# The low part of a weight used last in the projections and feed-forward products, and a doubled hand-over margin in the list scheduler

## The chip, the core and the metric

The kernel is one launch on one NeuronCore of a Trainium2 chip. Its engines are TensorE (PE for its matmuls, PEld for its weight loads), VectorE (DVE), ScalarE (ACT), GpSimd (POOL) and SyncE (SP), whose queue issues all of the kernel's transfers. The metric is the device time of the launch in microseconds (us); lower is better. A profiled execution also gives a span, from the first to the last instruction of the program.

## The reference

One decoder layer on 2048 tokens of width 1024 (DEPTH is 1, so only the first, gated-DeltaNet layer is computed):

```
proj = x @ w_in                       # q, k, v, z (8 heads of 128 each), 16 gate columns, 4 memory-query heads
qkv  = silu(causal_depthwise_conv(qkv)); q, k l2-normalised
o    = chunk_gated_delta_rule(q, k, v, g, beta)      # per head: a triangular solve per chunk, a state 128x128
o    = rms_norm(o) * silu(z);  m = memory_attention(mq, mem_k, mem_v)   # 256 memory tokens
x    = layer_norm(ALPHA * x + concat(o, m) @ w_out, ln1)
x    = layer_norm(ALPHA * x + square(relu(x @ w_ff1)) @ w_ff2, ln2)     # hidden width 4096
```

## The kernel before

**Arithmetic.** Each large product is made of three matmuls in a rounded fp32 type. An operand is split into a high part (a rounded copy, a CAST on ACT) and a low part (the original minus that copy, a subtraction on DVE). With `wh`, `wl` for a weight and `Thi`, `Tlo` for the transposed activations, one term of a product is Thi·wh + Tlo·wh + Thi·wl, all summed into the same PSUM bank. The low part of a weight is therefore ready only after its high part: transfer, CAST on ACT, subtraction on DVE. `hilo` and `hilo_in` (around line 465) do that for weights; the tiles come from a pool of 11 buffers with the tag `w`. The helper `mm3` issues the three matmuls in this order:

```
        nc.tensor.matmul(o, lh, rh, start=start, stop=False, **kw)
        nc.tensor.matmul(o, lh, rl, start=False, stop=False, **kw)
        nc.tensor.matmul(o, ll, rh, start=False, stop=stop, **kw)
```

**Stages.** The 2048 tokens go in four blocks of 512. In a block the mixer runs over ten steps: `dense` projects q, k, v, z of one head (accumulators `aq`, `ak`, `av`, `az`, each 24 matmuls of 512 columns, in `project`), `gdn_a` builds and inverts the chunk matrices (small plain-fp32 products `pkq`, `pq`, `pp`), `gdn_b` runs the state recurrence (`pc`, `po`) of the head before; `mem_proj` and `mem_attn` (`amq`, `sps`, `pmT`, `pmo`) do the memory heads. `out_proj` (accumulators `ao`) is interleaved at the end of the mixer. Then `norm1` normalises 128 tokens at a time (DVE, with a power on POOL), and `to_T` or `to_quads` transposes them (PE, tile `pt`) and splits them.

**Feed-forward.** The two feed-forward products (FF1, FF2; accumulators `af`) are done by a recursion of the Strassen kind: seven products of quarter size instead of eight, over sums and differences of quarters (`S1` to `S4`, `T1` to `T4`). Four groups of 1024 hidden units (`g`) each do FF1 and then FF2 for the block. In block 0 FF1 is plain (`ff1_tiles`, through `project`), and the sums of weights are made and kept in DRAM; in blocks 1 to 3 FF1 is `ff1_quads`, whose `step` does one of the seven products of 256 columns for two halves `i`. FF2 is the loop over `SEVEN` with the inner function `part(t, v)`; there the activations are the stationary operand (`xh`, `xl`, `hq`) and the weight is the moving one.

**Order.** The code above only records operations. `Recorder.issue` then plans: a list scheduler with one clock for each engine takes the recorded operation that can start first, ties by a priority that is the recording order (with hand-set shifts), and gives each an assumed duration. When an operation hands over to another engine, the reader is taken to be ready `LAT_FROM[e] + MARGIN` ns after the end of the writer, and a freed buffer is taken to be free as much later. `MARGIN` is 50. The planned start times only set the order in which the instructions are emitted on each engine; on the chip every engine runs its own list in order and waits on semaphores where a value is not there yet. Matmuls into the same bank stay in recorded order.

Of the kernel before, what the change touches and what calls it, by code (L numbers as in the profile page):

```python
# [14 lines left out]
P = 128  # L15
# [3 lines left out]
KT = D // P  # L19
# [13 lines left out]
RATE, FROM_SP, TO_SP = 330.0, 400, 400  # L33
LAT = {("PE", "PE"): 0, ("DVE", "DVE"): 120, ("ACT", "ACT"): 140, ("POOL", "POOL"): 100}
LAT_FROM = {"PE": 200, "DVE": 130, "ACT": 140, "POOL": 90, "SP": FROM_SP}
MARGIN = 50
SHIFT = 110
LATE = 600
PT3, PT2, PT1, PT4, PT5 = 0, 60, 30, 200, 130
# [28 lines left out]
class Ref:  # L68
# [58 lines left out]
    def part(self, *keys):  # L127
        return Ref(self.buf, self.shape, self.steps, frozenset(keys), self.p0)
# [223 lines left out]
def hybrid_layer(  # L352
# [24 lines left out]
    nc = tc.nc  # L377
# [59 lines left out]
    nc = rec  # L437
# [231 lines left out]
            nc.shift = 0  # L669

    def project(o, w, T, n=TB, t0=0):
        for k in range(KT):
            kk = [100 * k + t for t in range(t0 // P, (t0 + n) // P)]
            mm3(o, w[0][k], w[1][k], T[0][:, k, t0:t0 + n].part(*kk), T[1][:, k, t0:t0 + n].part(*kk),
                k == 0, k == KT - 1)


    mem_T = {}
# [515 lines left out]
    def ff_seven(b, ff1_tiles, ff1_quads, relu2, add, norm2):  # L1194
# [3 lines left out]
        for g in range(NS):  # L1198
            u0 = 4 * g
            X = [None] * 4  # L1200
# [72 lines left out]
            for n, (xn, wn, bn, on, (th, nh)) in enumerate(SEVEN[i] for i in order):  # L1273
                if not on:
                    banks[bn] = [bank("af2", ("ga%d" % t) if bn == "A" else "pb") for t in range(2)]
                w = [None, None]
                if b == NB - 1 and last and n == 5:
                    W = [rec.buf(tp, (P, 4, 1024), F32R, c, 1, "w") for c in ("Thi", "Tlo")]
                    spare.extend([x[:, i].part(("w", i)) for x in W] for i in range(4))

                def part(t, v):
                    if w[v] is None:
                        w[v] = as_rows(*(
                            hilo_in(tsc[u0 + v, wn]) if wn in (1, 2, 3, 4) else
                            hilo_in(fcp[u0 + v, wn]) if b else hilo(load_raw(row_part(u0 + v, wn)))))
                    for j in range(2):
                        k = 2 * v + j
                        h, l = X[k][xn]
                        mm3(banks[bn][t], h[:, t * P:(t + 1) * P], l[:, t * P:(t + 1) * P],
                            w[v][0][:, j], w[v][1][:, j], k == 0 and not on, k == 3, skip_group_check=on)  # L1290

                tail = last and n == len(SEVEN) - 1
                for v, t in ((0, 0), (1, 0), (0, 1), (1, 1)) if tail else ((0, 0), (0, 1), (1, 0), (1, 1)):
                    part(t, v)
                    if v:
                        add(2 * th + t, nh, banks[bn][t])
                        if tail:
                            norm2((t,), gb)
                if last and xn == "S1":
                    norm2((2, 3), gb)  # L1300
                if last and n < 4:
                    next_block(b + 1, n)
                if last and n == 5:
                    next_block(b + 1, 4)
# [46 lines left out]
    for b in range(NB):  # L1351
# [115 lines left out]
        def ff1_quads(vs, As, Bs, Cs, put):  # L1467

            out, held = {}, {}

            def step(v, n):
                wn, tn, bn, on = FF1_SEVEN[n]
                hi, lo = load_hilo(fhl[v, wn]) if (v, wn) in fhl else hilo_in((fsc if wn[0] == "S" else fac)[v, wn])
                hi, lo = (r.rearrange("p (a k f) -> p a k f", a=2, k=4) for r in (hi, lo))
                for i in range(2):
                    if bn == "A":
                        o, start = As[v, i][:, :256], not on
                    else:
                        o, start = (Bs if bn == "B" else Cs)[v][:, 256 * i:256 * i + 256], i == 0 and not on
                    for k in range(4):  # L1480
                        th, tl = quad_k(T1, tn, k)
                        for m, (a, x) in enumerate(((hi, th), (hi, tl), (lo, th))):
                            nc.tensor.matmul(o, a[:, i, k], x, start=start and k == 0 and m == 0,
                                             stop=k == 3 and m == 2, skip_group_check=True)
                    reads.append((v, n, i, o))

            def read(v, n, i, o):
                wn = FF1_SEVEN[n][0]
                if wn == "A12":
                    held[v, i] = o  # L1490
                    return
                if (v, i) not in out:
                    t, u = tok_tile("sq2"), tok_tile("ss4")
                    out[v, i] = t.rearrange("p (q f) -> p q f", q=4), u.rearrange("p (q f) -> p q f", q=4)
                a, st = out[v, i]
                sq = lambda q: a[:, q].part(q)
                ss = lambda q: st[:, q].part(q)
                sub = lambda o, x, y, op=ALU.subtract: nc.vector.tensor_tensor(out=o, in0=x, in1=y, op=op)
                if wn in ("A11", "S2", "S3"):
                    nc.scalar.copy(out=sq({"A11": 3, "S2": 1, "S3": 0}[wn]), in_=o)  # L1500
                    if wn != "A11":
                        return
                    o = held.pop((v, i))
                q = {"A11": 3, "S1": 0, "A22": 1, "S4": 2}[wn]
                if wn == "S4":
                    nc.scalar.activation(sq(q), o, AF.Relu)
                else:
                    nc.vector.tensor_tensor(out=sq(q), in0=sq(q), in1=o, op=ALU.add)
                    nc.scalar.activation(sq(q), sq(q), AF.Relu)
                nc.scalar.activation(sq(q), sq(q), AF.Square)  # L1510
                if wn == "S1":
                    put(v, i, ("A11", "A22"), a[:, 0:4:3].part(0, 3))
                elif wn == "A22":
                    sub(ss(0), sq(1), sq(3), ALU.add)
                    sub(ss(2), sq(0), sq(1))
                    sub(ss(1), ss(0), sq(0))
                    put(v, i, ("S3",), st[:, 2:3].part(2))
                    put(v, i, ("S1", "S2"), st[:, 0:2].part(0, 1))
                elif wn == "S4":
                    put(v, i, ("A12",), a[:, 2:3].part(2))  # L1520
                    sub(ss(3), sq(2), ss(1))
                    put(v, i, ("S4",), st[:, 3:4].part(3))

            order = [(v, n) for v in vs for n in range(7)]
            if len(vs) > 1:
                order.sort(key=lambda x: (x[1] > (x[0] == vs[0]), x[0], x[1]))
            reads = []
            for v, n in order:
                step(v, n)
                for q in reads:  # L1530
                    read(*q)
                reads.clear()
                if n == 6:
                    yield v
# [72 lines left out]
```

## Time and profile before

| | |
|---|---|
| median of 3 runs | 2855.46 us (2853.58, 2864.53, 2855.46) |
| the profiled execution | 2857.76 us |
| its span | 2855.8 us |
| PE, PEld busy in the span | 2817.9 us, 2420.0 us |
| DVE, ACT, POOL busy | 2341.8 us, 1648.5 us, 425.2 us |
| matmul records | 15869 |
| mean granted TensorE clock | 0.998 |

The profiled execution is 2.3 us above the median; 2.0 us of it lie outside its span. The profile's line for nearly every instruction is that of one helper (L335, where the recorded operations are emitted), so groups are told apart by the names of the tiles: `af<-wl,xh` is a matmul that writes `af` and reads `wl` and `xh`. The duration that a row gives for a matmul is its way through the pipeline; matmuls overlap, so the distance between two starts says what one costs in a row of them.

### The profile page before, as it was taken

The page shows a single profiled execution, that of the slowest core. Times are in us where ns is not written, and L with a number is a line of the kernel's source. Part 1 is how long each engine was busy: PE and PEld are TensorE (multiplying, and loading weights), DVE is VectorE, ACT ScalarE, POOL GpSimd, SP SyncE. Part 2 cuts the span into 40 slices and gives each one's busy share as a digit, 9 for nine tenths or more (in the row PEclk, how much of TensorE's full clock was granted, in tenths as well). Part 3 has the DMA queues.
Part 4 walks back from the last instruction along what each step waited for, and adds up shares of the span by engine and source line. Part 5 has one row for each costly group of instructions (what it writes and reads, how often), then busy time and mean ns, then how long its engine had stood idle before and what let it go on. Part 6 is the DMA issues. An engine that isn't in the chain of part 4 may idle for free. (4 is left out here: it accounts for less than half of the span.)

```text
span 2855.8 us, 47712 instructions
## 1 busy us (share of the span) xinstructions
PE 2817.9 (99%) x15869; PEld 2420.0 (85%) x15869; DVE 2341.8 (82%) x6188; ACT 1648.5 (58%) x4147; POOL 425.2 (15%) x1051
## 2 busy tenths in 40 slices
PE   9999999999999999999999999999999999999998
PEld 7888788888788888899988888889998888888997
DVE  8999989888889887777788986677788888577778
ACT  6677625555466663566645664256674666356664
POOL 2333200000133321000012321000002332000000
PEclk9999999999999999999999999999999999999999
DMA  8575569888877777655684434565577443465554
GB/s 300 209 264 188 176 220 312 297 283 270 299 259 257 237 257 266 218 187 188 217 270 152 133 122 148 210 207 188 188 236 250 132 141 121 166 237 177 188 188 177
DMA packets 200982, 609.59 MB, mean 213 GB/s; under 512 B 22560, under 2 KB 41376, under 8 KB 200352
## 3 DMA queue, kind: packets, MB, share of 16 engines
q1 hardware_dynamic: 200736, 606.55, 63.0%
q8 instruction: 125, 2.05, 0.3%
q14 instruction: 121, 0.99, 0.1%
HBM read 500.49 MB, written 127.99 MB: 220 GB/s over the span
## 5 line engine op out<-in xcount | busy, mean ns | idle before, releaser
L335 ACT CAST wh<-wl 128x1024 fp32r<-128x1024 f32 x334 | 349.7, 1048 | 246.2 <-DMA wl<-tsc 77.3
L335 DVE TENSOR_TENSOR wl<-wl,wh 128x1024 fp32r<-128x1024 f32 x334 | 400.0, 1219 | 62.2 <-ACT wh L335 62.1
L335 PE MATMUL af<-wh,xl 128*128 128x512 f32 x880 | 342.9, 390 | 1.3 <-DVE xl L335 1.3
L335 PE MATMUL af<-Thi,wh 128*128 128x256 f32 (+1 forms) x1056 | 323.5, 307 | 2.1 <-DVE tq L335 2.1
L335 PE MATMUL af<-Thi,wl 128*128 128x256 f32 (+1 forms) x1056 | 323.6, 307 | 1.3 <-DVE wl L335 1.3
L335 PE MATMUL af<-Tlo,wh 128*128 128x256 f32 (+1 forms) x1056 | 323.4, 306 | 0.0
L335 PE MATMUL af<-wl,xh 128*128 128x512 f32 x754 | 295.3, 392 | 3.6 <-DVE wl L335 3.5
L335 PE MATMUL af<-wh,xh 128*128 128x512 f32 x754 | 286.2, 390 | 2.3 <-ACT wh L335 2.2
L335 DVE SCALAR_TENSOR_TENSOR y<-y,af 128x512 f32<-128x512 f32 x224 | 151.0, 682 | 87.2 <-PE af L335 87.1
L335 PEld LDWEIGHTS af<-Thi,wh 128*128 128x128 f32 x1056 | 202.2, 192 | 12.3 <-DVE tq L335 2.8
L335 PEld LDWEIGHTS af<-Thi,wl 128*128 128x128 f32 x1056 | 202.4, 192 | 10.4 <-DVE wl L335 1.7
L335 PEld LDWEIGHTS af<-Tlo,wh 128*128 128x128 f32 x1056 | 202.4, 192 | 9.1
L335 PE MATMUL af<-Tx,wh 128*128 128x256 f32 x1152 | 209.3, 283 | 0.0
L335 ACT CAST wh<-wr 128x1024 fp32r<-128x1024 f32 (+1 forms) x132 | 136.9, 1038 | 121.9 <-DMA wr<-in_w_ff_dram 45.5
L335 PEld LDWEIGHTS af<-wh,xl 128*128 128x128 f32 x880 | 165.2, 188 | 35.8 <-DVE xl L335 1.7
L335 PEld LDWEIGHTS af<-Tx,wh 128*128 128x128 f32 x1152 | 179.8, 192 | 0.6 <-ACT sq L335 0.6
L335 PEld LDWEIGHTS af<-wl,xh 128*128 128x128 f32 x754 | 141.6, 188 | 38.5 <-DVE wl L335 9.9
L335 DVE TENSOR_TENSOR wl<-wr,wh 128x1024 fp32r<-128x1024 f32 (+1 forms) x132 | 158.5, 1203 | 16.7 <-ACT wh L335 12.6
L335 PEld LDWEIGHTS af<-wh,xh 128*128 128x128 f32 x754 | 141.4, 188 | 33.0 <-ACT wh L335 3.4
L335 PE MATMUL af<-Tx,wl 128*128 128x256 f32 x576 | 162.4, 283 | 0.0
L335 PE MATMUL ao<-wh,ch 128*128 128x512 f32 x384 | 153.0, 399 | 2.5 <-DVE y L335 1.0
L335 PE MATMUL ao<-wl,ch 128*128 128x512 f32 x384 | 155.3, 404 | 0.0
(316 smaller groups left out, 7693.0 us busy)
## 6 DMA issues: line engine op xcount, KB each, us to landing
wl<-tsc SPq DMA_DIRECT2D x128, 512.0 KB, 4.0
wh<-wsc SPq DMA_DIRECT2D x108, 512.0 KB, 5.3
wl<-wsc SPq DMA_DIRECT2D x108, 512.0 KB, 4.6
wl<-fsc SPq DMA_DIRECT2D x84, 512.0 KB, 3.4
wl<-fcp SPq DMA_DIRECT2D x68, 512.0 KB, 3.4
wr<-in_w_ff_dram SPq DMA_DIRECT2D x62, 512.0 KB, 5.0
wl<-fac SPq DMA_DIRECT2D x54, 512.0 KB, 3.4
wsc<-wh SPq DMA_DIRECT2D x36, 512.0 KB, 4.2
```

Source lines behind the costliest of these rows:

```text
L335: o.fn(*[res(a) for a in o.args], **{k: res(v) for k, v in o.kw.items()})
```

## The change

Three pieces of code now use the low part of a weight last. `project` does the 16 matmuls with `wh` for all eight k first, and then the 8 with `wl`. `part` in FF2 does the `wh` matmuls of both token tiles first (8), then the `wl` ones (4); in the last product of the kernel each token tile still goes by itself. `step` in FF1 of blocks 1 to 3 does the 16 `wh` matmuls of both halves `i`, then the 8 `wl` ones, and both results are read after that. `mm3` itself stays for `out_proj`, the memory keys and values and `pkq`. And `MARGIN` goes from 50 to 100, which moves the planned start of every operation behind a hand-over, and so the order on all engines.

```
-MARGIN = 50
+MARGIN = 100
...
     def project(o, w, T, n=TB, t0=0):
+        def rhs(hl, k):
+            return T[hl][:, k, t0:t0 + n].part(*[100 * k + t for t in range(t0 // P, (t0 + n) // P)])
         for k in range(KT):
-            kk = [100 * k + t for t in range(t0 // P, (t0 + n) // P)]
-            mm3(o, w[0][k], w[1][k], T[0][:, k, t0:t0 + n].part(*kk), T[1][:, k, t0:t0 + n].part(*kk),
-                k == 0, k == KT - 1)
+            nc.tensor.matmul(o, w[0][k], rhs(0, k), start=k == 0, stop=False)
+            nc.tensor.matmul(o, w[0][k], rhs(1, k), start=False, stop=False)
+        for k in range(KT):
+            nc.tensor.matmul(o, w[1][k], rhs(0, k), start=False, stop=k == KT - 1)
...
-                def part(t, v):
+                def part(t, v, lo):
...
-                        mm3(banks[bn][t], h[:, t * P:(t + 1) * P], l[:, t * P:(t + 1) * P],
-                            w[v][0][:, j], w[v][1][:, j], k == 0 and not on, k == 3, skip_group_check=on)
+                        if lo:
+                            mm(h, 1, end=k == 3)
+                        else:
+                            mm(h, 0, first=k == 0 and not on)
+                            mm(l, 0)
...
-                for v, t in ((0, 0), (1, 0), (0, 1), (1, 1)) if tail else ((0, 0), (0, 1), (1, 0), (1, 1)):
-                    part(t, v)
-                    if v:
+                for v, ts in ((0, (0,)), (1, (0,)), (0, (1,)), (1, (1,))) if tail else ((0, (0, 1)), (1, (0, 1))):
+                    for lo in (False, True):
+                        for t in ts:
+                            part(t, v, lo)
+                    for t in ts if v else ():
                         add(2 * th + t, nh, banks[bn][t])
...
+                for late in (False, True):
+                    for i in range(2):
...
+                            for m, (a, x) in enumerate(((lo, th),) if late else ((hi, th), (hi, tl))):
...
+                        if late:
+                            reads.append((v, n, i, o))
```

The instructions are the same in kind and number on every engine (14741 matmuls on PE); only their order differs. Three places show it.

PE at the start of the program, before: the rows from the last of the gate matmuls (`aab`) on. Ahead of them stand the matmuls of the first projection (`aq`), three for each k as the activations arrive, all but its last one.

```order
L335 MATMUL aab<-Thi,abw 32x512
L335 MATMUL aab<-Tlo,abw 32x512
L335 MATMUL aq<-Thi,wl 128x512
L335 MATMUL ak<-Thi,wh 128x512
L335 MATMUL ak<-Tlo,wh 128x512
L335 MATMUL ak<-Thi,wl 128x512
```

The same place now; ahead of it stand the 16 `wh` matmuls of `aq` and none of its `wl` ones.

```order
L335 MATMUL aab<-Thi,abw 32x512
L335 MATMUL aab<-Tlo,abw 32x512
L335 MATMUL aq<-Thi,wl 128x512 x7
L335 MATMUL pab<-ident,ab 128x32 x4
L335 MATMUL aq<-Thi,wl 128x512
L335 MATMUL ak<-Thi,wh 128x512
```

Seven low-part matmuls of `aq` move from among the arrivals of the activations to behind `aab`; before, six matmuls of `ak` stood between `aab` and the transposes `pab`.

PE at the first change from FF1 to FF2 of block 1, before. `af2_14008` and `af2_14027` are the banks of the two token tiles, `wh_13961` with `wl_13868` is FF2's first piece of weight, `wh_14001` its second.

```order
L335 MATMUL af2_14008<-wh_13961,xh_13690 128x512
L335 MATMUL af2_14008<-wl_13868,xh_13690 128x512
L335 MATMUL af2_14008<-wh_13961,xl_13702 128x512
L335 MATMUL af2_14008<-wh_13961,xh_13711 128x512
L335 MATMUL af2_14008<-wl_13868,xh_13711 128x512
L335 MATMUL af2_14008<-wh_13961,xl_13719 128x512
L335 MATMUL af2_14027<-wh_13961,xh_13690 128x512
```

And now (the banks are 14004 and 14016, the first piece is 13921 with 13864):

```order
L335 MATMUL af2_14004<-wh_13921,xh_13705 128x512
L335 MATMUL af2_14004<-wh_13921,xl_13714 128x512
L335 MATMUL af2_14004<-wh_13921,xh_13720 128x512
L335 MATMUL af2_14004<-wh_13921,xl_13728 128x512
L335 MATMUL af2_14016<-wh_13921,xh_13705 128x512
L335 MATMUL af2_14016<-wh_13921,xl_13714 128x512
L335 MATMUL af2_14016<-wh_13921,xh_13720 128x512
L335 MATMUL af2_14016<-wh_13921,xl_13728 128x512
L335 MATMUL af2_14004<-wl_13864,xh_13705 128x512
L335 MATMUL af2_14004<-wl_13864,xh_13720 128x512
L335 MATMUL af2_14016<-wl_13864,xh_13705 128x512
L335 MATMUL af2_14016<-wl_13864,xh_13720 128x512
```

The first use of a low part moves from the second place after the change of stage to the ninth; the second piece of weight is needed from the thirteenth matmul on in both.

DVE at the same change of stage, before: after the first piece's low part come the splits (`xl`) and sums (`ss4`) of FF1's last results (`sq2`), and behind them the second piece's low part, `wl_13902`.

```order
L335 TENSOR_TENSOR wl_13868<-wl_13868,wh_13961 128x1024
L335 TENSOR_TENSOR xl_13995<-sq2_13850,xh_13973 128x512
L335 TENSOR_TENSOR ss4_14005<-sq2_13838 128x256 x2
L335 TENSOR_TENSOR ss4_14005<-ss4_14005,sq2_13838 128x256
L335 TENSOR_TENSOR ss4_14018<-sq2_13850 128x256 x2
L335 TENSOR_TENSOR xl_14029<-ss4_14005,xh_14020 128x256
L335 TENSOR_TENSOR ss4_14018<-ss4_14018,sq2_13850 128x256
L335 TENSOR_TENSOR xl_14038<-ss4_14005,xh_14025 128x512
L335 TENSOR_TENSOR xl_14044<-ss4_14018,hq_14032 128x256
L335 TENSOR_TENSOR xl_14050<-ss4_14018,hq_14032 128x512
L335 TENSOR_TENSOR xl_14029<-sq2_13838,xh_14020 128x256
L335 TENSOR_TENSOR ss4_14005<-sq2_13838,ss4_14005 128x256
```

And now, from the first piece's low part, `wl_13864`, on; the second piece's is `wl_13903`.

```order
L335 TENSOR_TENSOR wl_13864<-wl_13864,wh_13921 128x1024
L335 TENSOR_TENSOR sq2_13847<-sq2_13847,af_13762 128x256
L335 TENSOR_TENSOR sq2_13857<-sq2_13857,af_13781 128x256
L335 TENSOR_TENSOR sq2_13847<-sq2_13847,af_13816 128x256
L335 TENSOR_TENSOR sq2_13857<-sq2_13857,af_13816 128x256
L335 TENSOR_TENSOR wl_13903<-wl_13903,wh_13952 128x1024
L335 TENSOR_TENSOR xl_13992<-sq2_13847,xh_13981 128x512
L335 TENSOR_TENSOR xl_14001<-sq2_13857,xh_13988 128x512
L335 TENSOR_TENSOR ss4_14012<-sq2_13847 128x256 x2
```

The second piece's low part now stands ahead of the splits and sums; before, it was the next row after the twelve shown.

DVE in the normalisation ahead of FF1 of block 1, before: from the last sum of `out_proj` into `y` to the end of the normalisation, whose result PE transposes next.

```order
L335 SCALAR_TENSOR_TENSOR y<-y,ao 128x512
L335 BN_STATS bn<-y 128x6
L335 TENSOR_TENSOR tq<-tq,tf 128x512
L335 TENSOR_TENSOR tq<-tf,tq 128x512
L335 BN_STATS bn<-y 128x6
L335 TENSOR_TENSOR tq<-tf,tq 128x512
L335 TENSOR_TENSOR Tlo<-tq,Thi 128x4x128
L335 BN_AGGR mv<-bn 128x2
L335 TENSOR_TENSOR tq<-tf,tq 128x512
L335 SCALAR_TENSOR_TENSOR y<-y,mv,l1g 128x512 x2
L335 SCALAR_TENSOR_TENSOR y<-y,rs,l1b 128x512 x2
```

And now:

```order
L335 SCALAR_TENSOR_TENSOR y<-y,ao 128x512
L335 BN_STATS bn<-y 128x6
L335 TENSOR_TENSOR tq<-tq,tf 128x512
L335 TENSOR_TENSOR tq<-tf,tq 128x512
L335 BN_AGGR mv<-bn 128x2
L335 TENSOR_TENSOR tq<-tf,tq 128x512
L335 SCALAR_TENSOR_TENSOR y<-y,mv,l1g 128x512
L335 TENSOR_TENSOR Tlo<-tq,Thi 128x4x128
L335 SCALAR_TENSOR_TENSOR y<-y,mv,l1g 128x512
L335 SCALAR_TENSOR_TENSOR y<-y,rs,l1b 128x512 x2
```

Between the last sum and the end of the normalisation stand two operations fewer: one `BN_STATS` comes ahead of the sum, and one `tq` comes after the normalisation.

More of the change, by code (lines that the diff above doesn't have):

```diff
@@ L1287, in part @@
                         k = 2 * v + j
-                        h, l = X[k][xn]
-                        mm3(banks[bn][t], h[:, t * P:(t + 1) * P], l[:, t * P:(t + 1) * P],
-                            w[v][0][:, j], w[v][1][:, j], k == 0 and not on, k == 3, skip_group_check=on)
-                tail = last and n == len(SEVEN) - 1
-                for v, t in ((0, 0), (1, 0), (0, 1), (1, 1)) if tail else ((0, 0), (0, 1), (1, 0), (1, 1)):
-                    part(t, v)
-                    if v:
+                        h, l = (x[:, t * P:(t + 1) * P] for x in X[k][xn])
+                        mm = lambda a, wi, first=False, end=False: nc.tensor.matmul(
+                            banks[bn][t], a, w[v][wi][:, j], start=first, stop=end, skip_group_check=True)
+                        if lo:
[3 more added lines that the diff above has]
+                            mm(l, 0)
+                tail = last and n == len(SEVEN) - 1
+                for v, ts in ((0, (0,)), (1, (0,)), (0, (1,)), (1, (1,))) if tail else ((0, (0, 1)), (1, (0, 1))):
[3 more added lines that the diff above has]
+                    for t in ts if v else ():
                         add(2 * th + t, nh, banks[bn][t])
@@ L1474, in step @@
                 hi, lo = (r.rearrange("p (a k f) -> p a k f", a=2, k=4) for r in (hi, lo))
[L1475 to L1485, printed above, removed]
+                for late in (False, True):
+                    for i in range(2):
+                        if bn == "A":
+                            o, start = As[v, i][:, :256], not on
+                        else:
+                            o, start = (Bs if bn == "B" else Cs)[v][:, 256 * i:256 * i + 256], i == 0 and not on
+                        for k in range(4):
+                            th, tl = quad_k(T1, tn, k)
+                            for m, (a, x) in enumerate(((lo, th),) if late else ((hi, th), (hi, tl))):
+                                nc.tensor.matmul(o, a[:, i, k], x, start=start and k == 0 and m == 0 and not late,
+                                                 stop=late and k == 3, skip_group_check=True)
+                        if late:
+                            reads.append((v, n, i, o))
             def read(v, n, i, o):
```

## The prediction

> **What bounds the kernel.** I read the page's first part, then who waited for whom on PE, then the timeline around the longest of those waits.
>
> ```profile
> span 2855.8 us, 47712 instructions
> PE 2817.9 (99%) x15869; PEld 2420.0 (85%) x15869; DVE 2341.8 (82%) x6188; ACT 1648.5 (58%) x4147; POOL 425.2 (15%) x1051
> ```
>
> TensorE is the bound: 99% busy, with a weight load for every matmul. The change neither adds nor removes a matmul, so only time in which PE stands can be won, and only new standing lost. PE's waits (waiting tile, releaser: idle us, times, longest):
>
> ```profile
> PE af L335 <- DVE wl L335: 4.8, 9, 0.8
> PE af L335 <- ACT wh L335: 2.2, 3, 0.7
> PE pt L335 <- DVE y L335: 2.1, 3, 0.9
> PE af L335 <- DVE tq L335: 2.1, 3, 0.7
> PE warm L335 <- POOL ident masks.py:199: 1.8, 1, 1.8
> PE pp L335 <- POOL X L335: 1.8, 2, 1.0
> PE ptq L335 <- ACT kd L335: 1.6, 1, 1.6
> PE af L335 <- DVE xl L335: 1.3, 1, 1.3
> ...
> PE ao L335 <- DVE y L335: 1.0, 1, 1.0
> PE ao L335 <- ACT ch L335: 0.9, 2, 0.5
> ...
> PE pkq L335 <- DVE Bc L335: 0.2, 1, 0.2
> ```
>
> There are 23 such rows, 40 waits, 26.4 us in all; 1.8 us of it is the launch. The idle time understates a wait, because a matmul's modelled duration reaches past the start of the next. The place that shows it is the first change from FF1 to FF2 in block 1:
>
> ```profile
> 1180.69 0.39 PE L335 MATMUL af<-wh,xl 128*128 128x512 f32 x1
> 1180.92 0.61 PE L335 MATMUL af<-wh,xh 128*128 128x512 f32 x2
> 1182.26 0.73 PE L335 MATMUL af<-wh,xh 128*128 128x512 f32 x2 [0.72 <-ACT wh L335]
> 1183.73 0.50 PE L335 MATMUL af<-wl,xh 128*128 128x512 f32 x1 [0.74 <-DVE wl L335]
> ```
>
> Starts of 512-column matmuls are 0.23 us apart when nothing is late (1180.69 to 1180.92). Two of them from 1180.92 should let the next start at 1181.38; it started at 1182.26, so the wait cost 0.88 us where 0.72 is shown. I add 0.16 us to each wait: 39 waits after the launch, 24.6 + 6.2 = 30.8 us. That is the most the waits that the view lists can give.
>
> **Low part last, in the feed-forward.** Here is what PE waited for:
>
> ```profile
> 1181.17 1.03 ACT L335 CAST wh<-wl 128x1024 fp32r<-128x1024 f32 x1
> 1182.46 1.22 DVE L335 TENSOR_TENSOR wl<-wl,wh 128x1024 fp32r<-128x1024 f32 x1
> ```
>
> The second piece's low part ends 1.5 us after its high part (1183.68 against 1182.20). With eight high-part matmuls first, PE has 8 x 0.23 = 1.8 us of work in that time, so a low part that is 1.5 us behind no longer stops it. The high part itself stays needed from the thirteenth matmul; but in the new DVE order its low part, and so its CAST on ACT before that, stands ahead of the group of splits, where it stood behind it. In FF1 of blocks 1 to 3 the cover is 16 matmuls of 0.12 us (rows below), 1.9 us; in `project` 16 as well. So the waits for `wl` (9) and `wh` (3) should mostly go: 7.0 us of idle time and 12 x 0.16 = 1.9 us, 8.9 at most. I take -7, because DVE is busy throughout the hand-over and some waits will come back as waits for `xl`; bounds -9 and 0.
>
> **The normalisation ahead of FF1.** These rows lie between the last `out_proj` sum and the transposes in block 1:
>
> ```profile
> 1133.34 0.68 DVE L335 BATCH_NORM_STATS2 bn<-y 128x6 f32<-128x512 f32 x1
> 1133.94 0.67 DVE L335 TENSOR_TENSOR tq<-tq,tf 128x512 f32<-128x512 f32 x1
> 1134.54 0.68 DVE L335 TENSOR_TENSOR tq<-tf,tq 128x512 f32<-128x512 f32 x1
> ...
> 1138.93 1.40 DVE L335 SCALAR_TENSOR_TENSOR y<-y,rs,l1b 128x512 f32<-128x512 f32 x2
> ```
>
> ```profile
> 1138.47 0.28 PE L335 MATMUL af<-Tlo,wh 128*128 128x256 f32 x1
> 1138.59 0.28 PE L335 MATMUL af<-Thi,wl 128*128 128x256 f32 x1
> 1139.73 1.38 PE L335 MATMUL pt<-ident,y 128*128 128x128 f32 x8 [0.86 <-DVE y L335]
> 1141.80 0.39 PE L335 MATMUL af<-Thi,wh 128*128 128x256 f32 x1 [0.69 <-DVE tq L335]
> ```
>
> DVE runs without a pause, and PE waits 0.86 us for its end. The new order has two operations of 0.60 us fewer there, 1.2 us. Against that, the transposes of the earlier tokens stand seven 256-column matmuls later on PE (7 x 0.12 = 0.84 us), and with them the copies on ACT that the `tq` rows read, so DVE may pause some 0.4 us that it did not. Net -0.8 us, in three blocks, each bounded by its idle time (2.1 us together): I take -2, bounds -2.6 (three times 0.86) and +1. The wait for `tq` behind the transposes (2.1 us) has no other matmul put in front of it in the new order and stays.
>
> **The clock.** After the stall of block 1 the granted clock halves, and in block 2 it does not (columns: stretch, PE busy and count, PEld, DVE, ACT, POOL, clock, DMA share, GB/s):
>
> ```profile
> 347.10:350.30 3.20, 3.20 (x11) 2.74 (x10) 1.83 (x6) 2.34 (x6) 1.31 (x6) 0.50 0.27 97
> 1142.40:1145.60 3.20, 3.20 (x17) 3.20 (x16) 3.20 (x9) 1.21 (x2) 0.00 (x0) 0.50 0.19 76
> 1838.80:1842.00 3.20, 3.20 (x27) 3.20 (x28) 3.20 (x9) 1.73 (x3) 0.00 (x0) 1.00 0.46 188
> ```
>
> At half clock 17 matmuls passed where 27 pass at full clock; two such stretches cost some 1.6 us each. Both follow a cluster of waits that is among those above. I take one of the two away, -1.6, bounds -3.2 and +1.6 (a third one).
>
> The Trainium skill (TensorE: Matmul & The Clock Gate, "Why this matters for your kernels") says that TensorE falls back to half rate after one idle window of about 3 us or more. By that rule neither stretch would be there, since no wait in the table above but the launch's is over 1.6 us long, and this term would be 0 and the time 1.6 us longer. The trace does not agree, and I go by the trace.
>
> **The margin, in the mixer.** The 13 rows of PE's waits from `pp` (1.8) down to `pkq` (0.2) that belong to the mixer and to `out_proj` sum to 9.5 us in 15 waits, 11.9 us with 0.16 each. A doubled margin makes the planner put more other matmuls into a hand-over: between `pc<-R,Y` and `pc<-vt,kd`, which is one trip through ACT, the order before has three large matmuls in 79 of 128 cases, and now four in 73. But the plan that results is another one everywhere, and its new places where PE has nothing to fill with are not in this trace. I take half away, -6, and for new waits +3 (a quarter of what the old plan had); bounds -12 and +12 (as many new ones, none of the old gone).
>
> **The start.** This costs. Before, PE used the time between the arrivals of the activations for the low part of `aq`:
>
> ```profile
> 6.91 0.39 PE L335 MATMUL aq<-Thi,wl 128*128 128x512 f32 x1
> 13.82 0.50 PE L335 MATMUL aq<-Tlo,wh 128*128 128x512 f32 x1
> 17.84 0.40 PE L335 MATMUL aq<-Thi,wl 128*128 128x512 f32 x1
> 18.08 0.39 PE L335 MATMUL ak<-Thi,wh 128*128 128x512 f32 x1
> 20.53 0.43 PE L335 MATMUL pab<-ident,ab 32*128 32x32 f32 x4 [0.65 <-ACT ab L335]
> ```
>
> ```profile
> 19.91 0.57 ACT L335 COPY ab<-aab 32x512 f32<-32x512 f32 x1
> ```
>
> The last arrival, at 13.82, is not earlier now, nor is `ab`, which stands behind the same CASTs in ACT's list. So at `pab` PE has done seven `wl` matmuls of `aq` in place of one and six of `ak`, and is behind by 7 x 0.23 = 1.6 us that nothing later gives back. +1.6, bounds +0.5 and +3.2 (half clock there as well).
>
> **Costed at nothing.** In FF1 of blocks 1 to 3 the result of the first half `i` comes 8 x 0.12 = 0.96 us later, close to the second, and in FF2 two sums into `y` come closer together. Both lie beside FF2's or the next product's matmuls: FF2 starts with results that are one or two products of 24 x 0.12 = 2.9 us old. If that cover is short it is the slower rival below. The high parts' buffers come free earlier, the low parts' no later, so no transfer moves back. The end of the kernel keeps the same operations on DVE behind the last matmul.
>
> **Sum.** -7 - 2 - 1.6 - 6 + 3 + 1.6 = -12.0 us. On the profiled execution, 2857.8, that is 2845.8; on the median, 2.3 us lower, 2843.5. I forecast 2843.5 us, -0.4%. About 0.5%, 14 us, is what a measurement of this kernel can tell from no change, so the forecast lies within it, near its lower edge.
>
> **Rivals.**
> - *Nearly all waits go.* Against +1.6 at the start stand 30.8 us and two half-clock stretches of 1.6 us, 34 us; less what arrives late at the start and the chain behind the transposes (some 4 us): -28, 2827. For it: every hop whose rows I compared has more work put between. Against it: DVE at 82% runs in order, so a late operation delays those behind it whatever the margin.
> - *The waits only move.* PE waits as much as before, at other places, and only `wl` and the start count: -7 + 1.6 gives 2850, and if those 7 us come back elsewhere too, 2857. For it: a plan made with assumed durations misses somewhere else.
> - *Slower: FF1's results come too late for FF2.* Twelve changes from FF1 to FF2 in blocks 1 to 3, each 0.96 us later because both halves are read at the end: +11.5, with the start +1.6 and one more half-clock stretch +1.6: +14.7, 2870. It decides where ACT and DVE need more than the 2.9 us of the last FF1 product to turn its forerunners into `xh` and `xl`. Against it: in the trace PE waits for `xl` only once, in block 0, where FF1 has no such halves.
> - *The change does nothing* can't be: the order differs on all engines.
>
> **Chances.** Forecast case (-5 to -20) 0.55, of which four in ten are past 14 us; nearly all go 0.14; only move 0.23; slower 0.08, three in four of it past 14 us. Faster by over 0.5%: 0.22 + 0.14 = 0.36. Slower: 0.06. Within: 0.58. For eight in ten the range runs from the first rival, 2827, to 2859, which takes in the waits that only move and leaves out most of the slower case. The forecast case's own range is 2835 to 2851.
>
> **What would show it.** Right: the row of PE's waits `af <- wl` falls from 4.8 to under 1, `pt <- y` to under 1, the total of 26.4 us to about 15; the start has PE idle between arrivals and `ak` begins about 1.6 us later; block 1 has no half-clock stretch. Wrong: new rows `af <- xl` or `af <- xh` of several us in blocks 1 to 3 (slower rival), or mixer waits as large as before under other names (they only moved).

## The result and the profile after

| | median us | runs | ratio to before, 95% interval |
|---|---|---|---|
| before | 2855.28 (2853.58 to 2864.53) | 6 | |
| after | 2835.22 (2834.53 to 2836.88) | 6 | 0.9925 [0.9912, 0.9938] |

The change makes the kernel 20.1 us faster, 0.7%. The forecast was -12 us, 2843.5, inside the bound of 0.5%; the measured gain lies beyond that bound, which the prediction gave a chance of 0.36. The time fell inside the range of 2827 to 2859 and on the lower edge of the forecast case's own, 2835 to 2851. The profiled execution took 2834.73 us (2857.76 before). In the experiments below, one execution of the kernel with MARGIN 200 ran at a granted clock of 0.574 and took 4506.6 us; it is left out of that kernel's figures.

The page of the changed kernel, first part:

```profile
span 2833.0 us, 47757 instructions
PE 2806.3 (99%) x15869; PEld 2422.0 (85%) x15869; DVE 2333.5 (82%) x6188; ACT 1636.6 (58%) x4147; POOL 425.4 (15%) x1051
```

The span is 22.8 us shorter. Only half of that is idle time: span less PE busy was 37.9 us and is 26.7, so 11.2 less. PE's busy time, for the same 15869 records, fell by 11.6.

Who PE waited for, after (waiting tile, releaser: idle us, times, longest):

```profile
PE af L335 <- DVE tq L335: 2.1, 3, 0.7
PE pt L335 <- DVE y L335: 1.9, 3, 0.6
...
PE af L335 <- PE af L335: 1.5, 3, 0.5
PE af L335 <- DVE y L335: 1.2, 2, 0.8
PE af L335 <- DVE xl L335: 0.9, 1, 0.9
...
PE af L335 <- ACT wh L335: 0.8, 2, 0.4
...
PE af L335 <- DVE wl L335: 0.2, 1, 0.2
```

The view has 20 rows, 31 waits, 15.8 us (23, 40 and 26.4 before). `af<-wl` went from 4.8 us to 0.2 and `af<-wh` from 2.2 to 0.8. New is `af<-PE af`, three times 0.5, one in each of blocks 1 to 3 early in FF1, where PE waits for matmuls of its own. It comes with the margin: the kernel with the margin alone (below) has the same row, 1.5 us in 3, the others with MARGIN 100 or 200 have two or three of these waits, and no kernel with MARGIN 50 has one.

The first change from FF1 to FF2 in block 1, where the two waits of 0.72 and 0.74 us stood:

```profile
1161.39 0.40 PE L335 MATMUL af<-wh,xh 128*128 128x512 f32 x1
...
1163.23 1.07 PE L335 MATMUL af<-wl,xh 128*128 128x512 f32 x4
1164.14 0.39 PE L335 MATMUL af<-wh,xh 128*128 128x512 f32 x1
...
1165.95 1.07 PE L335 MATMUL af<-wl,xh 128*128 128x512 f32 x4
```

Two groups of 12 matmuls take 1161.39 to 1166.86 without a bracket, 0.23 us each.

Where in the program the time went shows best by stage. A feed-forward stage begins where only `pt` and `af` matmuls follow, more than 60 in a row, and a mixer with its first `aq`. These are rows by stretch (us, then busy time and count of PE, PEld, DVE, ACT, POOL, then clock, DMA share, GB/s) for the mixer and the feed-forward of block 0. The stages are counted from PE's first instruction, which is 1.8 us into the span, so in both profiles the rows are cut 1.8 us ahead of the stage's first matmul. Before:

```profile
0.00:416.80 416.80, 406.27 (x2187) 338.22 (x2188) 374.12 (x1201) 259.64 (x751) 115.89 (x277) 1.00 0.66 229
416.80:758.00 341.20, 336.66 (x1574) 278.84 (x1573) 289.96 (x494) 176.11 (x247) 7.26 (x16) 1.00 0.85 285
```

After:

```profile
0.00:408.10 408.10, 403.02 (x2186) 339.15 (x2187) 371.98 (x1200) 259.16 (x751) 116.24 (x277) 1.00 0.67 233
408.10:745.50 337.40, 335.00 (x1573) 278.49 (x1572) 291.37 (x500) 175.72 (x249) 8.97 (x16) 1.00 0.85 291
```

The second column less the third is PE's idle time in the stage: in the mixer of block 0 it fell from 10.53 to 5.08 us, and the busy time there by 3.25. That stage alone gives 8.7 of the 22.8 us; some 1.6 of it is a stretch at half clock (at 347 us) that is gone. The same cuts in every profile of this study are used below (M mixer, F feed-forward, us). The last column says in which stages the profile has a half-clock stretch of 3.4 us, worth some 1.6 us each; the last section is about them.

| kernel | M0 | F0 | M1 | F1 | M2 | F2 | M3 | F3 to the end | half clock |
|---|---|---|---|---|---|---|---|---|---|
| before | 416.8 | 341.2 | 372.1 | 327.1 | 370.1 | 325.4 | 369.8 | 331.5 | M0, F1 |
| after | 408.1 | 337.4 | 369.2 | 324.0 | 370.1 | 324.1 | 369.0 | 329.3 | none |
| margin alone | 413.3 | 341.5 | 373.2 | 325.6 | 367.2 | 325.4 | 367.1 | 331.3 | F0, M1 |
| low part last alone | 410.5 | 336.1 | 371.8 | 322.8 | 370.9 | 322.8 | 371.1 | 329.2 | none |
| after, margin 200 | 413.0 | 341.1 | 370.5 | 324.4 | 367.5 | 323.5 | 367.6 | 329.9 | M0, F0, F1 |
| after, start as before | 408.1 | 340.2 | 368.3 | 324.9 | 369.0 | 324.0 | 370.2 | 329.4 | F0, F1 |
| `project` alone | 411.3 | 337.4 | 372.3 | 325.4 | 370.3 | 325.4 | 369.9 | 331.5 | none |
| FF2 alone | 415.4 | 341.1 | 371.1 | 322.8 | 369.9 | 322.6 | 370.5 | 329.3 | M0 |
| FF1 alone | 417.3 | 340.9 | 370.5 | 332.3 | 371.1 | 332.0 | 370.6 | 338.4 | M0 twice, F1, F2, F3 |
| FF1 and FF2 | 416.5 | 341.8 | 371.4 | 323.9 | 370.9 | 324.2 | 370.8 | 329.2 | M0, F2 |
| `project` and FF2 | 409.6 | 335.7 | 373.2 | 322.5 | 369.9 | 322.6 | 370.2 | 329.2 | none |
| FF1 by half alone | 415.8 | 341.1 | 371.4 | 329.1 | 370.0 | 326.1 | 370.3 | 332.2 | M0, F1 twice |
| after, FF1 edit undone | 408.9 | 338.2 | 369.2 | 323.1 | 369.0 | 322.6 | 369.0 | 328.5 | none |
| after, FF1 by half | 409.0 | 337.2 | 369.9 | 322.6 | 369.7 | 322.6 | 369.4 | 328.5 | none |

### The profile page after: what moved, and what is told of

Same layout as the page of the kernel before. It is cut to its first block, busy times and chain, and to the rows that moved or that the text cites. A ratio compares the mean times of both kernels' runs of the same rounds, so it can differ in the third digit from the quotient of the medians.

```text
span 2833.0 us, 47757 instructions
## 1 busy us (share of the span) xinstructions
PE 2806.3 (99%) x15869; PEld 2422.0 (85%) x15869; DVE 2333.5 (82%) x6188; ACT 1636.6 (58%) x4147; POOL 425.4 (15%) x1051
## 4 chain that ended last, share of the span: by engine, by line
PE 87%; DVE 7%; DMA 2%; ACT 1%; issue 1%; SPq 0%; POOL 0%; DVEq 0%; ACTq 0%; POOLq 0%
PE af L335 40%; PE ao L335 7%; PE ak L335 6%; PE av L335 6%; PE az L335 6%; PE aq L335 6%; PE pc L335 3%; PE amq L335 3%; DVE y L335 2%; PE po L335 2%; PE pkq L335 2%; PE pq L335 1%; PE pp L335 1%; PE sps L335 1%; PE pmo L335 1%
## 5 line engine op out<-in xcount | busy, mean ns | idle before, releaser
L335 PE MATMUL af<-wh,xh 128*128 128x512 f32 x754 | 294.3, 392 | 2.0 <-DVE y L335 1.2
L335 PE MATMUL af<-Thi,wh 128*128 128x256 f32 (+1 forms) x1056 | 291.9, 306 | 3.5 <-DVE tq L335 2.1
L335 PE MATMUL af<-Tlo,wh 128*128 128x256 f32 (+1 forms) x1056 | 292.1, 306 | 0.0
L335 PE MATMUL af<-wl,xh 128*128 128x512 f32 x754 | 219.0, 390 | 0.2 <-DVE wl L335 0.2
L335 DVE SCALAR_TENSOR_TENSOR y<-y,af 128x512 f32<-128x512 f32 x224 | 143.8, 680 | 88.7 <-PE af L335 88.5
L335 PE MATMUL af<-Thi,wl 128*128 128x256 f32 (+1 forms) x1056 | 172.4, 306 | 0.0
L335 PEld LDWEIGHTS af<-Thi,wl 128*128 128x128 f32 x1056 | 149.4, 191 | 8.7
L335 PE MATMUL ao<-wh,cl 128*128 128x512 f32 x384 | 155.0, 405 | 0.2 <-DVE cl L335 0.2
L335 PE MATMUL af<-Tx,wh 128*128 128x256 f32 x1152 | 150.5, 283 | 0.0
L335 PEld LDWEIGHTS af<-Tx,wh 128*128 128x128 f32 x1152 | 143.6, 192 | 0.0
```

The lines of the kernel that those rows point to most:

```text
L335: o.fn(*[res(a) for a in o.args], **{k: res(v) for k, v in o.kw.items()})
```

## Experiments

Ratios are to the kernel before, run beside each on the same chip (medians of before 2855.74, 2856.62 and 2855.64 us in the three groups of four). Low part last goes by its three places: `project`, FF2's `part`, FF1's `step`.

### The two halves of the change

The kernel before with only

```
-MARGIN = 50
+MARGIN = 100
```

> MARGIN at 100 and the three matmuls in the old order. Theory A (the two edits add: low part last takes away the waits for weights in the feed-forward, some 8 us, the margin the waits in the mixer and short ones): 2843 to 2847, about 10 us under the kernel before, with PE's wait af <- wl still at 3 us or more. Theory B (the margin alone does it, since more work between hand-overs covers the weights' low parts too): 2835 to 2838, af <- wl under 1 us. Theory C (low part last does it alone): 2852 to 2857.

The changed kernel with only

```
-MARGIN = 100
+MARGIN = 50
```

> Low part last and MARGIN at 50. Theory A: 2844 to 2849, af <- wl under 1 us, the mixer's waits (pp, pc, pq, ao, sps and the like) at some 9 us as in the kernel before. Theory B: 2853 to 2857. Theory C: 2835 to 2838.

Margin alone: 2847.5 us, 0.9969 [0.9959, 0.9979]. Low part last alone: 2838.47, 0.9942 [0.9927, 0.9957]. So -8.2 and -17.3, which would add to -25.5; together they give -20.1. No theory has both: the first had the margin alone nearly right (2843 to 2847) and low part last alone 6 us too slow (2844 to 2849), the third the reverse (2852 to 2857 and 2835 to 2838). Low part last carries most of the gain, and the margin adds 3 us to it where it gives 8 alone; those 3 us are not firm, since the intervals of the two ratios, [0.9927, 0.9957] and [0.9912, 0.9938], overlap. The waits for `wl` are not what the margin takes away; with it alone that row is higher than the 4.8 before:

```profile
PE af L335 <- DVE wl L335: 6.3, 7, 2.0
```

### More margin

The changed kernel with

```
-MARGIN = 100
+MARGIN = 200
```

> The changed kernel with MARGIN at 200. If more margin only puts more work between hand-overs, the short waits go on falling: 2830 to 2834. If the margin has passed what the hand-overs really take, the plan now holds work back and fills with later work, and the chains at the stages' ends come later: 2836 to 2845.

2840.97 us (three executions), 0.9946 [0.9926, 0.9966]: in the range of the second case, and 5.8 us above MARGIN 100. M2 and M3 are shorter than with 100 (367.5 and 367.6 against 370.1 and 369.0), but M0 is 413.0 and F0 341.1, 8.6 us together over the changed kernel. Three half-clock stretches, which the changed kernel has not, make up some 4.8 us of the 5.8, so it is not shown that the larger margin is worse apart from where they fall, nor that the ends of the stages are the reason.

### The start as before

The changed kernel, with the first projection of the program in the old order:

```
-    def project(o, w, T, n=TB, t0=0):
+    def project(o, w, T, n=TB, t0=0, old=False):
...
+    if old:
+        for k in range(KT):
+            mm3(o, w[0][k], w[1][k], rhs(0, k), rhs(1, k), k == 0, k == KT - 1)
+        return
...
+            project(a, w, T, old=b == 0 and w is w0)
```

> The changed kernel, but the very first projection (aq of head 0 in block 0) takes its three matmuls for each k in the old order. If the start costs what was forecast for it, this is 1.6 us faster than the changed kernel; by the starts in its trace (ak's seventh matmul at 21.61 against 20.89) 0.7 us: 2833.6 to 2834.5. Rival: another plan from there on moves the time by more than that, either way, by 2 us or more.

2837.48 us, 0.9938 [0.9923, 0.9953]: 2.3 us slower than the changed kernel where 0.7 to 1.6 us less were expected; the rival, 2 us or more either way by another plan, fits. Its last matmul of the third head's `az` starts at 92.0 us, against 94.1, so the start does cost 2 us as far as that. But its M0 is 408.1 as well: by the end of the stage the lead is gone. And it has two half-clock stretches that the changed kernel has not (below), 3.3 us. What undoing the start is worth apart from the plan and the clock is not settled by this run.

### Low part last at one place

Each is the kernel before with one of the three edits. `project` alone:

```
...
+    for k in range(KT):
+        nc.tensor.matmul(o, w[0][k], rhs(0, k), start=k == 0, stop=False)
+        nc.tensor.matmul(o, w[0][k], rhs(1, k), start=False, stop=False)
+    for k in range(KT):
+        nc.tensor.matmul(o, w[1][k], rhs(0, k), start=False, stop=k == KT - 1)
```

> The kernel before with the low part last in `project` alone; FF1 of blocks 1 to 3, FF2 and MARGIN = 50 as before. Theory P (each place gives back its own waits, the sum of the places is the 17 us of the low part last alone): the gain lies where `project` is used. Between before and the low-part-last kernel the mixer of block 0 became 6.3 us shorter and FF of block 0 (whose FF1 goes through `project`) 5.1 us shorter, of which 1.8 us are two waits af<-Thi,wl; so 2855.5 - 8 = 2847 (2844 to 2850), block 0 shorter by 6 to 9 us, blocks 1 to 3 within 1 us. Theory Q (any other order of recording shuffles the plan, and what comes out is luck): the time is anywhere within 2855 +- 6, and the mixers of all four blocks change by 1 to 4 us with either sign.

FF2 alone:

```
...
+for lo in (False, True):
+    for t in ts:
+        part(t, v, lo)
...
```

> The kernel before with the low part last in FF2's `part` alone. Theory P: the waits af<-wh and af<-wl behind an xh of FF2 go: 2.1 us by starts in each of blocks 1 to 3 and about 2 us in block 0, and with the wait at 1142 not touched one half-clock stretch may stay: -8, 2847.5 (2845 to 2850), FF of blocks 1 to 3 each 2 us shorter, the mixers unchanged. Theory Q: FF of blocks 1 to 3 shorter too, but the mixers differ by 1 to 4 us each.

FF1 alone:

```
+for late in (False, True):
+    for i in range(2):
...
+        if late:
+            reads.append((v, n, i, o))
```

> The kernel before with the low part last in FF1's `step` of blocks 1 to 3 alone. Theory P: the kernel before has no wait of FF1 for wl in blocks 1 to 3, so 0 to -2: 2853.5 to 2855.5, or +3 where the halves read late delay FF2 by 1 us in each block. Theory Q: 2855 +- 6.

FF1 and FF2, the last two edits together:

> The kernel before with the low part last in FF1's `step` and FF2's `part`, not in `project`. Theory P: the sum of the two alone, and 17 us less what `project` alone gives: -9 to -10, 2846 (2843 to 2849), with FF of blocks 1 to 3 at 322.8 us each as in the low-part-last kernel and the mixer of block 0 at 416.8 as before. Theory Q: no such sum, off by over 4 us from the two single ones.

| | median us | ratio | against before |
|---|---|---|---|
| `project` alone | 2847.18 | 0.9971 [0.9960, 0.9981] | -9.4 |
| FF2 alone | 2846.39 | 0.9970 [0.9958, 0.9982] | -10.2 |
| FF1 alone | 2877.62 | 1.0078 [1.0063, 1.0093] | +21.0 |
| FF1 and FF2 | 2849.26 | 0.9975 [0.9965, 0.9985] | -7.4 |

`project` and FF2 came out in the ranges that the theory of places said, and at their places: `project` in M0 (-5.5) and F0 (-3.8), FF2 in F1 to F3 (-4.3, -2.8, -2.2). Some of this is the clock: about 1.6 us of M0 with `project`, and of F1 with either, are a half-clock stretch that before has and these profiles have not. In block 0, where some 2 us were expected of FF2 too, F0 stays at 341.1. Against the theory of luck, the stages that an edit does not touch mostly stay within 1 us.

`project` does not give back its own waits alone, though. Its two for `wl` in F0 (0.77 and 0.52 us) are gone, but FF2 of block 0 waits longer for its own, so that the row is no smaller than the 4.8 before:

```profile
PE af L335 <- DVE wl L335: 5.1, 8, 1.6
```

With FF2 alone the row `af<-wh` is gone from PE's waits, and the one for `wl` keeps three in block 0, two of them those of `project`:

```profile
PE af L335 <- DVE wl L335: 2.0, 3, 0.8
```

FF1 alone is 16 us above the highest time that either theory allowed (2861). FF1 and FF2 together came to 2849.26, at the upper end of the first theory's 2843 to 2849, but not as the sum of the two single edits: +21.0 and -10.2 would make +10.8. With FF1 alone F1 to F3 are 5.2, 6.6 and 6.9 us longer, and it has five half-clock stretches, one in each of these three stages; before has two. Its waits of PE (`af<-wh` was 2.2 in 3, `af<-wl` 4.8 in 9):

```profile
PE af L335 <- ACT wh L335: 12.5, 11, 1.3
PE af L335 <- DVE wl L335: 7.7, 14, 0.8
```

The timeline of that kernel behind the second change from FF1 to FF2 in block 1 (at 1254.64), PE:

```profile
1260.11 0.61 PE L335 MATMUL af<-wh,xh 128*128 128x512 f32 x2
1262.02 0.74 PE L335 MATMUL af<-wh,xh 128*128 128x512 f32 x2 [1.29 <-ACT wh L335]
1263.34 0.50 PE L335 MATMUL af<-wl,xh 128*128 128x512 f32 x1 [0.59 <-DVE wl L335]
```

And ACT ahead of it:

```profile
1249.66 0.42 ACT L335 ACTIVATE sq<-sq 128x256 f32<-128x256 f32 x1 [2.14 <-DVE sq L335]
1249.98 1.03 ACT L335 CAST wh<-wl 128x1024 fp32r<-128x1024 f32 x1
...
1257.56 1.03 ACT L335 CAST wh<-wl 128x1024 fp32r<-128x1024 f32 x1
...
1259.97 2.94 ACT L335 CAST wh<-wl 128x1024 fp32r<-128x1024 f32 x3
```

ACT first stands 2.14 us for a sum that needs an FF1 result. Then, between the CASTs at 1249.98 and 1257.56, it does the activations and splits of both halves in one train, and the next weights come as three CASTs in a row from 1259.97, the second of which ends at 1262. PE stands from 1260.7 for it. In the kernel before the same CASTs come one at a time, and the second begins 0.7 us ahead of the change, which is at 1258.65 there, where with FF1's edit it begins 2.9 us behind it:

```profile
1253.90 1.03 ACT L335 CAST wh<-wl 128x1024 fp32r<-128x1024 f32 x1
...
1257.96 1.04 ACT L335 CAST wh<-wl 128x1024 fp32r<-128x1024 f32 x1
...
1261.22 1.04 ACT L335 CAST wh<-wl 128x1024 fp32r<-128x1024 f32 x1
```

The transfers are not what is late. Paired with the CASTs in order, those of the weights cast at 1257.56 and 1259.97 landed at 1252.13 and 1254.31, more than 5 us earlier; before, the CASTs at 1257.96 and 1261.22 follow landings at 1256.48 and 1259.23. So the late half does cost, not through `xh` or `xl` but through FF2's weights, which stand behind it in ACT's queue. With FF2's edit beside it, nearly all of this is gone (F1 332.3 to 323.9): FF1's edit then costs 2.9 us instead of 21.0. Why FF2's order makes the plan put those CASTs early again was not tried apart.

### FF1's low part last, half by half

The kernel before, with 8 `wh` and then 4 `wl` matmuls inside each half `i`, so that the first half ends when it did:

```
 for i in range(2):
...
+    for late in (False, True):
+        for k in range(4):
+            th, tl = quad_k(T1, tn, k)
+            for m, (a, x) in enumerate(((lo, th),) if late else ((hi, th), (hi, tl))):
...
```

> The kernel before with FF1's low part last within each half `i` (8 matmuls with wh, 4 with wl, then the same for the other half), so that the first half's result comes as early as before. FF1's edit alone, over both halves, gave +21. Theory H1 (the first half's result that comes 0.96 us late is the cause: ACT and DVE get both halves' results together, and the CAST of FF2's weight stands behind them): 2855 (2851 to 2859), FF of block 1 at 326 to 328 and the waits af<-ACT wh back from 12.5 to 2 or 3 us. Theory H2 (the low part last in FF1 is itself the cause, since FF2's weights are then taken later from the pool): 2870 to 2878, and those waits stay over 8 us.

2860.99 us, 1.0020 [1.0011, 1.0029]: +5.4, where FF1 over both halves gave +21.0. F2 and F3 are back at 326.1 and 332.2. The late first half is thus the cause of most of the loss. The 5 us left are above the expected range. The two profiles are only 2.0 us apart, all of it in F1, which has two half-clock stretches where before has one (1.6 us); the rest of the 5 is not in them. In its waits `af<-wh` is down to nothing that the view lists, and

```profile
PE af L335 <- DVE y L335: 3.8, 5, 0.8
```

is new, for which neither theory has a reason.

### Without FF1's edit, and with it half by half

The kernel before with the edits of `project` and FF2, MARGIN 50:

> The kernel before with the low part last in `project` and in FF2's `part`, not in FF1's `step`; MARGIN = 50. Theory P (the places add): `project` alone gave -9.4 and FF2 alone -10.2 against the same runs of before, 2856.6, so -19.6: 2837 (2834 to 2840), with the mixer of block 0 at 410.5 to 411.5 and FF of blocks 1 to 3 at 322.8, 322.6, 329.3. Theory S (the two share one gain, since all three places together gave only -17): -13 to -15, 2842.

The changed kernel with FF1's `step` as before (MARGIN 100):

```
-for late in (False, True):
-    for i in range(2):
+for i in range(2):
...
+    reads.append((v, n, i, o))
```

> The same with MARGIN = 100, which is the changed kernel without its edit of FF1. Theory H (the edit of FF1 is a loss that the other two hide: FF of block 1 is 322.8 with FF2 alone and 323.9 with FF1 added, and 324.0 in the changed kernel): 1.2 us in each of three blocks better than the changed kernel, 2831.5 (2829 to 2834). Theory N (the edit of FF1 costs nothing beside FF2's): 2835 to 2837.

The changed kernel with FF1 half by half, the edit shown above:

> The changed kernel with FF1's low part last within each half, as in the run by halves. Theory H1: FF of blocks 1 to 3 1 us shorter each (the new wait of af for PE's own af goes, 0.64 us in each block): 2832 (2829 to 2834). Theory N (FF1's order does nothing beside FF2's): 2835 +- 2.

| | median us | ratio |
|---|---|---|
| `project` and FF2, margin 50 | 2836.55 (2834.59 to 2838.38) | 0.9933 [0.9920, 0.9945] |
| the same, margin 100 | 2831.98 (2829.73 to 2833.38) | 0.9915 [0.9902, 0.9929] |
| after, FF1 by half | 2831.24 (2830.54 to 2832.26) | 0.9914 [0.9900, 0.9927] |

The places add: -9.4 and -10.2 make -19.6, measured -19.1. FF1's edit takes 1.8 us of it away at margin 50 (-17.3 with all three), and 3.6 at margin 100 (-20.1 against -23.7). Both versions without the late half have medians 3 to 4 us below the changed kernel's, and F1 shorter by 0.9 and 1.4 us, F2 by 1.5, F3 by 0.8, about as the first theory said; not for its reason, though, since the new wait `af<-PE af`, which belongs to the margin, is still there in both (1.4 and 1.5 us). The runs of neither overlap those of the changed kernel (2834.53 to 2836.88), the intervals of the ratios do: better by 3 or 4 us is likely, and these two are the fastest of the study.

## Why the prediction was right, and where its sum was wrong

- **The bound and the sign.** Right. PE is the bound, its standing shrank, and the total of its waits came to 15.8 us where 15 was said. From the launch on that is 24.6 to 14.0 us of idle time, with 0.16 us for each of 9 waits fewer -12.0, the forecast to a tenth. That is partly luck, since the terms it was added up from were off both ways, and the spans of the two profiles are 22.8 us apart: the other 10.8 us are in no row of waits. Of the signs that were named, `af<-wl` and the half-clock stretch of block 1 came as said; `pt<-y` is 1.9, not under 1.
- **Low part last, -7.** Mis-sized; the step that failed. FF2 gave -10.2 alone, at the waits that the prediction named. `project`, which the prediction let count only where PE waited for `wl`, gave -9.4, and -5.5 of it in the mixer of block 0, where the view before has no wait for `wl` in a projection. There PE's idle time fell by 3.3 us, in waits of other names (10.53 us in before's row, 7.28 with `project` alone):

```profile
0.00:411.30 411.30, 404.02 (x2186) 338.13 (x2187) 372.04 (x1201) 258.69 (x751) 123.00 (x277) 1.00 0.66 231
```

  With 1.6 us taken off for each half-clock stretch, M0 is between 408.1 and 411.4 in all eight profiles with `project`'s edit and between 413.3 and 415.2 in the six without. The largest of these waits shows how a low part stops PE under another name. Before, PE:

```profile
37.45 0.47 PE L335 MATMUL aq<-Thi,wh 128*128 128x512 f32 x1
...
37.79 0.48 PE L335 MATMUL aq<-Tlo,wh 128*128 128x512 f32 x1
38.41 0.44 PE L335 MATMUL pt<-ident,ym 128*128 128x128 f32 x2
40.45 0.66 PE L335 MATMUL ptq<-ident,cq 128*128 128x128 f32 x4 [1.60 <-ACT kd L335]
40.86 0.47 PE L335 MATMUL aq<-Thi,wl 128*128 128x512 f32 x1
```

```profile
39.48 1.19 DVE L335 TENSOR_TENSOR wl<-wr,wh 128x1024 fp32r<-128x1024 f32 x1
```

  The wait is listed under `ptq`. But `aq` has begun, its third matmul needs the low part that DVE ends at 40.67, and matmuls of one bank keep their order: so none of the other `aq` matmuls can fill the time. With `project` alone twelve of them stand there, and `ptq` waits for nothing:

```profile
39.48 0.47 PE L335 MATMUL aq<-Thi,wh 128*128 128x512 f32 x1
...
42.31 0.60 PE L335 MATMUL ptq<-ident,cq 128*128 128x128 f32 x4
...
43.69 1.08 PE L335 MATMUL aq<-Thi,wl 128*128 128x512 f32 x4
```

  With the margin alone the order there is as before, and the wait is 1.47 us. The prediction had put this row, `ptq<-kd`, down to the margin. The other waits of M0 that `project` takes away (`pp<-X` 1.8 us, most of `ao<-y` 1.0) were not followed in this way, and some small ones are new.
- **FF1's halves, costed at nothing.** Wrong for the edit alone (+21.0), of the right order beside FF2's (+2 to +4). The slower rival had the place and the cause, a first half that is read late at the changes from FF1 to FF2; it named `xh` and `xl` as the victims, and it was FF2's weights. Its sum, twelve changes of 0.96 us and more, 2870, is within 8 us of the 2877.6 of FF1 alone by chance, since it counts another delay. What kept it from happening is FF2's edit beside it; the prediction had trusted to the length of the last product.
- **The margin in the mixer, -6 + 3.** About right: on top of low part last it gives -3.2 by the medians. By stage it is -7.9 in the four mixers and +3.9 in the four feed-forwards, so the mixers gain more than was said and the price lies elsewhere than in the mixer; 1.5 of it are the waits `af<-PE af`. That the total fits is luck. As a gain of its own it would be -8.2.
- **The clock, -1.6.** Both stretches went, not one: about -3.3.
- **The normalisation, -2.** About -0.4. The chain of DVE in block 1 is shorter as read from the order, 1118.76 to the transposes at 1123.96 us, 5.2, against 6.4. But the `BN_STATS` that left the chain went ahead of the last sum, and the sum came later. PE and DVE after:

```profile
1116.32 0.39 PE L335 MATMUL ao<-wh,cl 128*128 128x512 f32 x1
...
1123.96 1.27 PE L335 MATMUL pt<-ident,y 128*128 128x128 f32 x7 [0.63 <-DVE y L335]
```

```profile
1116.13 0.69 DVE L335 BATCH_NORM_STATS2 bn<-y 128x6 f32<-128x512 f32 x1
...
1118.05 0.68 DVE L335 SCALAR_TENSOR_TENSOR y<-y,ao 128x512 f32<-128x512 f32 x1
1118.76 0.69 DVE L335 BATCH_NORM_STATS2 bn<-y 128x6 f32<-128x512 f32 x1
```

  and before:

```profile
1131.64 0.39 PE L335 MATMUL ao<-wh,cl 128*128 128x512 f32 x1
```

  From the last `ao` matmul to the sum it was 1.10 us (1131.64 to 1132.74) and is 1.73; from the same matmul to the transposes 8.09 and 7.64. The prediction began its chain at the sum, a step too late. It also took one block for three: the wait is 0.86 us only in block 1, 0.62 in blocks 2 and 3, before and after.
- **The start, +1.6.** `ak` begins 2.15 us later than before (20.23 against 18.08), with the seven low-part matmuls of `aq` where they were said to be:

```profile
17.82 1.77 PE L335 MATMUL aq<-Thi,wl 128*128 128x512 f32 x7
19.52 0.43 PE L335 MATMUL pab<-ident,ab 32*128 32x32 f32 x4
...
20.23 0.40 PE L335 MATMUL ak<-Thi,wh 128*128 128x512 f32 x1
```

  But `pab` comes 1.0 us earlier (19.52 against 20.53), since it stands behind fewer matmuls. "Nothing later gives back" did not hold: the run with the old start is 2.1 us ahead at the third head and level at the end of the stage.
- **What was not in the sum.** PE's busy time fell by 11.6 us with the same matmuls. 3.3 of it are the clock, 1.4 the 0.16 us of 9 waits; some 7 are left. Distances from start to start, each less the median for neighbours of the same shapes and accumulators, show a part: excesses between 60 and 150 ns, too short for the view of waits, were 756, 66.3 us, and are 711, 61.1 us. The figures shift with what is taken as the same kind of neighbours (3.5 to 5.2 us less in three ways), and the rest of the 7 us is not traced. The prediction saw that idle time understates a wait, and then counted only waits that have a row. The range had no term for them either; it held because the rival in which nearly all waits go reached 16 us further down.

## What to carry to other kernels

Using last the operand that is ready last is worth trying at each accumulation by itself. An accumulation that stops early at a late operand cannot fill other hand-overs, and the wait is then listed under the name of the one it failed to fill. The question at each place is who reads the result: where an accumulator ends later, the price can fall on whatever stands behind its reader in that engine's queue, here a weight's CAST that has nothing to do with it. Edits that give a gain together should be run one by one; this change held a loss of 2 to 4 us beside gains of 9 and 10. And where the bound engine is 99% busy, half of what is won may lie inside its busy time, as here, and in no row of waits.

## What the runs showed of the hardware

Half-clock stretches follow a window in which PE was in part idle, not one in which it stood: from 12 us on, the longest single wait in any of the 14 profiles is 1.96 us. Those in mid-run all have a length of 3.413 us, and within a run they start a whole number of such lengths apart: before 346.976 and 1142.281, 233.0 lengths. In the one at 1142.3 the starts of matmuls of 256 columns are 0.213 us apart instead of 0.12, 16 of them, which makes 1.5 us. Cut into windows of that grid, the 14 profiles (12 to 2800 us) have 20 half-clock stretches. They follow 15 of the 17 windows in which PE was busy under 0.55 of the time, 4 of 12 between 0.55 and 0.60, 1 of 26 to 0.67, and none above. The bounds are rough, since ends of matmuls are modelled. So whether a cluster of waits costs 1.6 us more depends on how the grid falls over it. Before, ahead of the stretch at 1142.3, and the same place with the old start, ahead of one at 1128.4:

```profile
1138.90:1142.30 3.40, 1.78 (x12) 1.34 (x13) 3.38 (x9) 1.69 (x3) 0.00 (x0) 1.00 1.03 404
```

```profile
1125.00:1128.40 3.40, 1.99 (x14) 1.33 (x14) 3.38 (x9) 1.67 (x3) 0.00 (x0) 1.00 1.02 418
1128.50:1131.70 3.20, 3.20 (x17) 3.20 (x16) 3.20 (x9) 1.24 (x3) 0.00 (x0) 0.50 0.29 117
```

In the changed kernel the same two waits (0.63 and 0.69 us, the same as with the old start) fall into two windows, and the clock stays:

```profile
1120.60:1124.00 3.40, 2.77 (x24) 2.56 (x23) 3.40 (x8) 1.68 (x4) 1.47 (x2) 1.00 1.00 341
1124.00:1127.40 3.40, 2.62 (x19) 2.17 (x20) 3.38 (x9) 2.47 (x5) 0.00 (x0) 1.00 1.02 417
```

The Trainium skill (TensorE: Matmul & The Clock Gate, "What's actually happening") says that the window is 3413 ns long and runs freely; these traces agree. It gives an idle window as the condition for half rate; here the 20 stretches followed windows with PE busy 0.43 to 0.66 of the time.
